# Normalising with scalar_tensor_tensor in place of tensor_scalar while GpSimd adds, in a matmul with batch normalisation

## The chip, the cores and the metric

The kernel runs on one core of one Trainium2 chip. The metric is the device time of an execution in microseconds (us). Most kernels here ran several times, in rounds with the kernel before on the same chip. The profiled execution has a span, from the first to the last instruction, that is about 2 us shorter than the time reported for it. SBUF and PSUM are the core's two on-chip memories; in the code, names that end in `_ps` lie in PSUM, where TensorE's results land, and the other tiles lie in SBUF. Positions such as "at 161.26" are us from the start of that span.

A run counts as fast unless it lies over 1.5% above the fastest of its kernel.

## The reference

```python
y = np.matmul(x, weight)                        # 16 x 512 rows, K = 1024, N = 768
mean = np.mean(y, axis=(0, 1), keepdims=True)   # per column, over all 8192 rows
var = np.var(y, axis=(0, 1), keepdims=True)
y_norm = (y - mean) / np.sqrt(var + eps)
return (gamma * y_norm + beta).astype(np.float32)
```

No output can be written before its column's statistics over all rows are known.

## The kernel before

The 768 columns are six tiles of 128. The first three tiles are finished first. Their outputs are then produced while TensorE still multiplies for the fourth, fifth and sixth. In that stretch, roughly 133 to 182 us, the engines share the work like this (a block is 1024 rows of a tile; in the fourth tile VectorE and ScalarE each normalise one half of it):

- TensorE: the remaining matmuls, with the transposes of finished output slotted between them one by one, in a fixed order.
- VectorE: batch statistics of each new block (`bn_stats`), the product of the first three tiles with their scale (`norm_rows`), and half of the normalising of the fourth tile (`norm` with "dve").
- GpSimd: the addition of the shift for the first three tiles (`shift_rows`), which reads two tensors in SBUF.
- ScalarE: copies out of PSUM and the other half of the fourth tile's normalising (`norm` with "act").

```python
def norm_rows(c, s):                      # VectorE, first three tiles
    ...
    seq(nc.vector.tensor_mul(             # the scale lies in PSUM
        o_sb, yrow[c][:, s:s + 2], aff[0][:, None, :].to_broadcast([P, 2, NA]),
    ))

def shift_rows(c, s):                     # GpSimd, first three tiles
    o_sb = ost["row", c, s]
    seq(nc.gpsimd.tensor_add(o_sb, o_sb, sum1[:, None, :].to_broadcast([P, 2, NA])))

def norm(nt, c, eng):                     # y = y * scale + shift, in place
    if eng == "act":
        ...
    else:
        seq((nc.vector if eng == "dve" else nc.gpsimd).tensor_scalar(
            y(nt, c), y(nt, c), scale[:, nt:nt + 1], shift[:, nt:nt + 1],
            op0=ALU.mult, op1=ALU.add,
        ))

def outputs(nt, t0, step):                # blocks of 1024 rows of tile nt
    for b in range(C // 2):
        tb = t0 + step * b
        ...
        for i in range(2):
            at(tb - 2.2 + 0.5 * i, norm, nt, 2 * b + i, "act" if tb < tr + 2.0 and i == 0 else "dve")
        ...                               # transposes, copy out, store
```

`seq` keeps each engine's instructions in the order of their planned times. `tr + 2.0` is, in planned time, shortly after GpSimd's last add.

## Time and profile before

| | before |
|---|---|
| time, median of the first three runs | 219.95 us (219.61 to 220.23) |
| span of the profiled execution | 217.6 us, granted TensorE clock 0.985 of full speed |
| busy: TensorE, VectorE, ScalarE, GpSimd | 92%, 72%, 56%, 62% |
| tensor_scalar of 128x512 (L382) | 43 of them, median 0.407 us, longest 3.38 |
| GpSimd's add of 128x768 (L289) | 24 of them, mean 1.87 us |

TensorE sets the pace over most of the kernel, VectorE between 157 and 176 us. An instruction that waits for a port is shown as busy for the whole wait. So the waits for GpSimd are not in the idle times at all, but in durations far above the median of the same instruction.

### The profile page before, as it was taken

The page shows a single profiled execution, that of the slowest core. Times are in us where ns is not written, and L with a number is a line of the kernel's source. Part 1 is how long each engine was busy: PE and PEld are TensorE (multiplying, and loading weights), DVE is VectorE, ACT ScalarE, POOL GpSimd, SP SyncE. Part 2 cuts the span into 40 slices and gives each one's busy share as a digit, 9 for nine tenths or more (in the row PEclk, how much of TensorE's full clock was granted, in tenths as well). Part 3 has the DMA queues.
Part 4 walks back from the last instruction along what each step waited for, and adds up shares of the span by engine and source line. Part 5 has one row for each costly group of instructions (what it writes and reads, how often), then busy time and mean ns, then how long its engine had stood idle before and what let it go on. Part 6 is the DMA issues. An engine that isn't in the chain of part 4 may idle for free.

```text
span 217.6 us, 3451 instructions
## 1 busy us (share of the span) xinstructions
PE 200.3 (92%) x1178; PEld 104.9 (48%) x1178; DVE 155.8 (72%) x263; ACT 121.2 (56%) x227; POOL 134.2 (62%) x153
## 2 busy tenths in 40 slices
PE   7997999999999999999999999999999979997900
PEld 2452555554544565645656545444444435554600
DVE  3222978887978789998654369988899999728900
ACT  2001463645543466645666414967866689976950
POOL 8887686878684699953558304999995963000000
PEclk9999999999999999999999999999999999999985
DMA  5999999999999999993000000897877989999998
GB/s 70 156 196 187 191 196 196 197 197 196 196 189 195 197 196 196 196 197 49 0 5 0 0 0 0 305 348 293 304 286 293 332 274 370 338 347 284 282 345 243
DMA packets 70161, 43.75 MB, mean 201 GB/s; under 512 B 4096, under 2 KB 69632, under 8 KB 70144
## 3 DMA queue, kind: packets, MB, share of 16 engines
q0 software_dynamic: 34624, 18.36, 61.6%
q1 hardware_dynamic: 35520, 25.18, 35.8%
q8 instruction: 9, 0.15, 0.3%
q14 instruction: 8, 0.07, 0.1%
HBM read 36.71 MB, written 25.17 MB: 284 GB/s over the span
## 4 chain that ended last, share of the span: by engine, by line
PE 75%; DVE 8%; DMA 5%; POOL 3%; issue 3%; ACT 2%; ACTq 1%; POOLq 0%
PE y_ps L196 39%; PE y_ps L186 29%; PE o_ps L398 5%; DMA w_sb<-in_weight_dram 3%; DMA ring<-in_x_dram 2%; DVE stats L316 2%; DVE y_sb L382 2%; DVE ring L283 2%; POOL w_sb L149 2%; DVE o_sb L283 1%; ACT o_sb L411 1%; POOL ring L162 1%; PE y_ps L330 1%; PE a_ps L272 1%; PE tot_ps L232 1%
## 5 line engine op out<-in xcount | busy, mean ns | idle before, releaser
L196 PE MATMUL y_ps<-xT_sb,w_sb 128*128 128x512 bf16 (+1 forms) x484 | 117.6, 381 | 1.6 <-DMA w_sb<-in_weight_dram 1.3
L196 PEld LDWEIGHTS <-w_sb 128*128 128x128 bf16 x484 | 45.9, 96 | 59.3 <-issue 3.1
L343 ACT CAST y_sb<-y_ps 128x512 bf16<-128x512 f32 x59 | 34.5, 585 | 53.7 <-DVE stats L316 50.7
L186 PE MATMUL y_ps<-w_sb,xT_sb 128*128 128x384 bf16 x384 | 63.4, 326 | 0.0
L316 DVE BATCH_NORM_STATS2 stats<-y_ps 128x6 f32<-128x512 f32 x58 | 39.3, 685 | 19.9 <-PE y_ps L196 19.9
L162 POOL DMA_DIRECT2D ring<-in_x_dram x72 | 45.2, 633 | 11.9 <-DVE xT_sb L174 6.5
L186 PEld LDWEIGHTS <-xT_sb 128*128 128x128 bf16 x384 | 37.5, 98 | 25.6
L212 POOL TENSOR_TENSOR sum<-sum,sq_sb 128x384 f32<-128x384 f32 x38 | 38.0, 1001 | 18.4 <-ACT sq_sb L208 17.1
L174 DVE STREAM_TRANSPOSE xT_sb<-ring 128x1024 f32<-128x1024 f32 (+1 forms) x34 | 39.5, 1168 | 12.8 <-DMA ring<-in_x_dram 12.8
L398 PE MATMUL o_ps<-ident,y_sb 128*128 128x128 bf16 x240 | 38.2, 219 | 3.6 <-DVE y_sb L382 2.5
L289 POOL TENSOR_TENSOR ring<-ring,sum 128x768 f32<-128x768 f32 x17 | 31.1, 1864 | 13.1 <-ACT sum L274 12.1
L215 DVE TENSOR_TENSOR sum<-y_ps,sum 128x384 f32<-128x384 f32 x48 | 26.1, 544 | 14.4 <-ACT sq_sb L208 13.4
L208 ACT ACTIVATE sq_sb<-y_ps 128x384 f32<-128x384 f32 x48 | 23.4, 492 | 15.2 <-PE y_ps L186 11.6
L221 ACT CAST y_sb<-y_ps 128x384 bf16<-128x384 f32 x48 | 22.9, 476 | 7.3 <-DVE sum L215 7.0
L411 ACT CAST ring<-o_ps 128x1024 f32<-128x1024 bf16 (+1 forms) x24 | 22.5, 951 | 4.2 <-PE o_ps L398 2.7
L398 PEld LDWEIGHTS <-y_sb 128*128 128x128 bf16 x240 | 19.4, 97 | 8.6 <-DVE y_sb L382 3.3
L382 DVE TENSOR_SCALAR y_sb<-y_sb,scale,shift 128x512 bf16<-128x512 bf16 x43 | 22.0, 565 | 0.0
L283 DVE TENSOR_TENSOR ring<-y_sb,a_ps 128x768 f32<-128x768 bf16 x17 | 15.9, 937 | 0.0
L289 POOL TENSOR_TENSOR o_sb<-o_sb,sum 128x768 f32<-128x768 f32 x7 | 13.2, 1880 | 2.9 <-DVE o_sb L283 2.9
L377 ACT ACTIVATE y_sb<-y_sb,shift,scale 128x512 bf16<-128x512 bf16 x17 | 13.5, 816 | 0.0
L155 PE MATMUL idle_ps<-idle_sb 128*128 128x512 bf16 x38 | 11.0, 456 | 1.2 <-DVE idle_sb L103 1.2
L411 ACT CAST o_sb<-o_ps 128x512 f32<-128x512 bf16 x16 | 7.9, 679 | 0.3 <-PE o_ps L398 0.3
(62 smaller groups left out, 50.1 us busy)
## 6 DMA issues: line engine op xcount, KB each, us to landing
ring<-in_x_dram POOLq DMA_DIRECT2D x56, 256.0 KB, 8.6
out_dram<-ring SPq DMA_DIRECT2D x25, 384.0 KB, 3.0
out_dram<-ring SPq DMA_DIRECT2D x16, 512.0 KB, 5.1
out_dram<-o_sb SPq DMA_DIRECT2D x16, 256.0 KB, 3.7
out_dram<-o_sb SPq DMA_DIRECT2D x7, 384.0 KB, 3.4
ring<-in_x_dram POOLq DMA_DIRECT2D x16, 128.0 KB, 5.3
w_sb<-in_weight_dram POOLq DMA_DIRECT2D x8, 96.0 KB, 4.6
w_sb<-in_weight_dram POOLq DMA_DIRECT2D x4, 192.0 KB, 5.6
```

Of the source, the lines that this page charges most:

```text
L162: seq(nc.gpsimd.dma_start(x_bf[32 * i:32 * i + 32], src[:, :, KQ * i:KQ * (i + 1)]))
L174: seq(nc.vector.transpose(dst[:, half, :, jw0:jw1], src[:, :, jw0:jw1]))
L186: seq(nc.tensor.matmul(y_ps, xT[c][:, jw, s * P:(s + 1) * P, e], w_sb[:, jw, e, 0:NA], start=(jw == 0 and e == 0), stop=(jw == JW - 1 and ...
L196: seq(nc.tensor.matmul(y_ps, w_sb[:, jw, e, nt * P:(nt + 1) * P], xT[c][:, jw, q0 * QR:q1 * QR, e], start=(jw == 0 and e == 0 and q0 == 0) ...
L212: seq(eng.tensor_add(acc, acc, py.pop(("sq", c, s))))
L215: seq(nc.vector.tensor_add(sum1, py["row", c, s][:, 0:NA], sum1))
L289: seq(nc.gpsimd.tensor_add(o_sb, o_sb, sum1[:, None, :].to_broadcast([P, 2, NA])))
L316: seq(nc.vector.bn_stats(stats_of(nt)[:, i, :], py[nt, c]))
L343: seq(nc.scalar.copy(y(nt, c), py.pop((nt, c))))
L382: seq((nc.vector if eng == "dve" else nc.gpsimd).tensor_scalar(y(nt, c), y(nt, c), scale[:, nt:nt + 1], shift[:, nt:nt + 1], op0=ALU.mult, ...
L398: seq(nc.tensor.transpose(dst, src, ident))
L411: seq(nc.scalar.copy(o_sb, src))
```

## The change

While GpSimd adds, a VectorE tensor_scalar waits for it. The prediction takes the tensor_scalar to run in a fast mode (0.40 us for 512 columns) and says where that comes from. The intent of the change is to leave that mode: the same arithmetic is written as a scalar_tensor_tensor, with the shift, one value per row, broadcast along the 512 columns as a second tensor.

```diff
+        elif eng == "dve1":
+            seq(nc.vector.scalar_tensor_tensor(
+                y(nt, c), y(nt, c), scale[:, nt:nt + 1],
+                shift[:, nt:nt + 1].to_broadcast([P, CH]), op0=ALU.mult, op1=ALU.add,
+            ))
 ...
-  at(tb - 2.2 + 0.5 * i, norm, nt, 2 * b + i, "act" if tb < tr + 2.0 and i == 0 else "dve")
+  at(tb - 2.2 + 0.5 * i, norm, nt, 2 * b + i, "dve" if tb > tr + 2.0 else "dve1" if i else "act")
```

Eight instructions change their form. No engine's order changes.

## The prediction

> **What bounds the kernel now.** The time before is 219.95 us; the profiled execution spans 217.6 us, and all positions below are us in that span. I read the page first: TensorE is busy in every slice from 10 to 199 us, VectorE is at nine tenths or more in the five slices from about 158 to 185 us, and the chain names PE for 75% and DVE for 8%. So TensorE paces the kernel, and VectorE must pace it for a stretch. The chain in order of time says where (start, duration, what):
>
> ```profile
> 154.79 2.05 PE y_ps L196 x9
> ...
> 161.34 1.58 DVE y_sb L382
> 162.92 1.64 issue
> ...
> 175.71 0.51 DVE mv L350
> ...
> 177.93 0.72 ACT y_sb L377
> 178.65 0.05 issue
> 178.69 0.23 PE o_ps L398
> ```
>
> The chain is on VectorE from 156.86 to 176.2 us, goes through the statistics aggregate (L350) to ScalarE and returns to TensorE at 178.69. From there it stays on TensorE, with no gap, to 199.37, where the last statistics begin. The "issue" of 1.64 us behind L382 is no issue: it lies inside one tensor_scalar, as the timelines of VectorE and GpSimd show (start, duration):
>
> ```profile
> 161.26 3.38 DVE L382 TENSOR_SCALAR y_sb<-y_sb,scale,shift 128x512 bf16<-128x512 bf16 x1
> 166.03 1.62 DVE L382 TENSOR_SCALAR y_sb<-y_sb,scale,shift 128x512 bf16<-128x512 bf16 x1
> 171.96 0.45 DVE L382 TENSOR_SCALAR y_sb<-y_sb,scale,shift 128x512 bf16<-128x512 bf16 x1
> 176.66 1.23 DVE L382 TENSOR_SCALAR y_sb<-y_sb,scale,shift 128x512 bf16<-128x512 bf16 x1
> ```
> ```profile
> 160.86 1.84 POOL L289 TENSOR_TENSOR o_sb<-o_sb,sum 128x768 f32<-128x768 f32 x1
> 162.65 1.84 POOL L289 TENSOR_TENSOR ring<-ring,sum 128x768 f32<-128x768 f32 x1
> 165.67 1.83 POOL L289 TENSOR_TENSOR o_sb<-o_sb,sum 128x768 f32<-128x768 f32 x1 [1.18 <-DVE o_sb L283]
> ```
>
> The same instruction takes a median of 0.407 us (its line's own view). The first one ends at 164.64, which is 0.15 after the second add's end (162.65 + 1.84 = 164.49); the next at 167.65, again 0.15 after 165.67 + 1.83 = 167.50. So a tensor_scalar that meets a GpSimd add waits for that add's end and then needs 0.15 us. The first one even let a second, already queued add go ahead. TensorE's own waits between 150 and 200 us show what all this can cost (total, times, longest):
>
> ```profile
> PE o_ps L398 <- ACT y_sb L377: 1.2, 2, 0.9
> PE o_ps L398 <- DVE y_sb L382: 0.8, 2, 0.5
> ```
>
> That is 1.97 us in four gaps (0.30, 0.50, 0.23, 0.94), all from 167 to 178.7.
>
> **What the skill says.** The Trainium skill, "SBUF — State Buffer", section "Who interferes with whom", says that VectorE and GpSimd share one pair of ports under an exclusive lock; a tensor_scalar in a two-port mode takes it, and so does a VectorE instruction with two SBUF inputs when the GpSimd instruction reads SBUF. The first half agrees with the lines above. For the second half the kernel before has a witness, the VectorE add of squares (L212), whose two inputs are both in SBUF. I looked for those that meet GpSimd's adds of the same line:
>
> ```profile
> 84.23 0.55 DVE L212 TENSOR_TENSOR sum<-sum,sq_sb 128x384 f32<-128x384 f32 x1
> 89.43 0.77 DVE L212 TENSOR_TENSOR sum<-sum,sq_sb 128x384 f32<-128x384 f32 x1
> 94.81 1.10 DVE L212 TENSOR_TENSOR sum<-sum,sq_sb 128x384 f32<-128x384 f32 x1
> ```
> ```profile
> 86.62 3.17 POOL L212 TENSOR_TENSOR sum<-sum,sq_sb 128x384 f32<-128x384 f32 x3
> 92.32 3.18 POOL L212 TENSOR_TENSOR sum<-sum,sq_sb 128x384 f32<-128x384 f32 x3
> ```
>
> Eight of the ten take 0.54 to 0.55 us. The two that start inside a GpSimd add end at 90.20 and 95.91, both 0.41 after GpSimd's end (89.79, 95.50). It is the same wait, and the 0.41 is the pass over 384 columns. "Vector Engine (DVE) Microarchitecture Reference", section "5.1 Performance modes — why throughput varies by op and dtype", enables the fast modes for copy, cast, tensor_scalar and tensor_tensor; scalar_tensor_tensor isn't in that list, and packing wants 16-bit operands throughout, while the broadcast shift is fp32. I take one column per cycle. No run shows that yet, as the scalar_tensor_tensors of before have one to three columns.
>
> **The change part by part.** It adds and removes no instruction. The queue orders of the two kernels are equal on all engines but for the form of eight VectorE instructions: i=1 of blocks 0 to 6 of the fourth tile, and i=1 of block 0 of the fifth, which also falls before the time test. In the trace of before these are the tensor_scalars at 161.26, 166.03, 169.90, 171.96, 173.80, 176.66 and two of the three merged at 179.31. They hold 6.9 us of waiting: (3.38 - 0.4) + (1.62 - 0.4) + (0.68 - 0.4) + 0.05 + 0.05 + (1.23 - 0.4) + (1.93 - 0.4). The change means to remove it, by leaving the two-port mode. It gives in1 a second SBUF stream instead, so I expect the wait to stay.
>
> Cost of the new form: tensor_tensor takes 0.544 us for 384 columns (L215) and 0.937 for 768 (L283), 1.02 ns a column, so 512 columns take 0.544 + 128 x 1.02 ns = 0.675 us free, against 0.40. Blocked, it ends 0.41 + 0.13 = 0.54 after GpSimd's add, against 0.15: 0.39 more.
>
> Then in VectorE's order, with an add of 1.83 us, and GpSimd's next add kept waiting while the new instruction holds the lock:
> Block 0: GpSimd's adds to 164.49 are as before; end 165.03 in place of 164.64, so +0.39.
> Block 1: its add (165.67) waits for the VectorE product in front, so it is itself 0.39 late; end +0.39 more, +0.78.
> Block 2: likewise, +1.17, 171.75. The GpSimd add behind it, which ran from 170.39 to 172.26, now starts its pass at about 171.75 and ends at 173.5.
> Block 3: before it lost only 0.05. Now it asks at about 173.15 and ends at 173.5 + 0.54 = 174.05 in place of 172.41, +1.64.
> Block 4: GpSimd's next add ends at about 174.05 + 1.8 = 175.85; end 176.4 in place of 174.25, +2.15.
> The aggregate (L350) thus starts at 177.8 in place of 175.64.
> Block 5: about 180.5 in place of 177.89; the last two end near 185 in place of 181.57, +3.3.
>
> On the path: block 0's delay mostly fits the slack of TensorE, whose transposes reach that data at about 165.0. Block 2's comes through whole (TensorE waits for it at 170.64), and the aggregate's +2.15 comes through ScalarE's queue to TensorE's restart: 178.69 becomes 180.8. Later blocks: the second half of block 6 is wanted at 183.15 + 2.15 = 185.3 and is there at about 184.9, so it just fits. TensorE has no gap from the restart to the last statistics, so +2.15 reaches them. Behind them lies a tail of fixed length: DMA is idle from 200.5 to 202.5 and then moves the last 16 stores. Sum: 219.95 + 2.1 = 222.05, rounded to 222.0.
>
> **The rivals.** First, no contention: with the shift read as one value a row, the second port may not count. Then each of the eight takes 0.68 and VectorE gains up to 6.9 - 8 x 0.275 = 4.7 us. But TensorE's gaps are only 1.97 us, and DMA is full from 180 to 200 us, so the end gains 1 to 2 us: 218 to 219. For it speaks the intent; against it the two blocked L212 adds. I give it 0.14.
> Second, the delay is absorbed: VectorE idles over 5 us between 188 and 196 and can catch up, which would leave 220 to 220.5. Against it: TensorE, not VectorE, carries the path after 178.69. I give it 0.12.
> Third, worse: a new instruction loses to two queued adds, as block 0's did (1.8 us each), or block 6 comes too late: 223.5 to 225. Before, four of the first five asked before the next add was ready, by as little as 0.08 us, so the order can tip. I give it 0.1.
>
> **Range and chances.** The main case has 0.64, at 221.3 to 222.8. With the rivals' weights 8 in 10 lie in 219.0 to 223.4. The 2% bounds are 215.55 and 224.35: faster would need more than TensorE's gaps hold, 0.01; slower needs the third rival in full, 0.04.
>
> **What would show it.** Right: no new instruction under 0.65 us; those that meet an add end about 0.54 after its end; the aggregate near 177.8, TensorE's restart near 180.8, its gaps near 4.1 us in all. Wrong at the root: instructions of 0.68 us lying inside GpSimd adds, with neither engine longer. Wrong in the size: waits as said, but TensorE's gaps grow by well under 2 us, or a new instruction spans two adds.

## The result, and the profile after

| | before | after |
|---|---|---|
| median of six runs each | 219.41 us | 221.64 us |
| lowest to highest | 218.31 to 220.23 | 220.56 to 222.64 |
| span of the profiled execution | 217.6 us | 220.2 us |

The ratio is 1.0104, with a 95% interval of 1.0059 to 1.0149. A ratio here is the mean time of one kernel's fast runs over that of the other's of the same rounds, so not quite the ratio of the medians. The change made the kernel slower by about 1%.

The chain of the changed kernel in order of time (start, duration, what) takes the same road as before:

```profile
154.88 2.50 PE y_ps L196 x11
...
161.90 1.58 DVE y_sb L383
163.47 2.05 issue
165.52 0.94 DVE o_sb L283
...
178.28 0.51 DVE mv L350
...
180.50 0.72 ACT y_sb L377
181.22 0.05 issue
181.26 0.23 PE o_ps L404
```

The two profiled executions are already 0.55 us apart before the first changed instruction: it starts at 161.81, against 161.26. That difference comes from the loading stage (the first batch statistics start at 20.91 against 20.37) and belongs to no changed line. Each comparison of positions has to take it off. The aggregate (L350) starts at 178.21 against 175.64, TensorE restarts at 181.26 against 178.69, and the last statistics start at 201.96 against 199.39. Each is 2.57 us later, or 2.02 us without the offset.

The new instructions on VectorE's timeline, and the GpSimd adds that they meet (start, duration):

```profile
161.81 3.79 DVE L383 SCALAR_TENSOR_TENSOR y_sb<-y_sb,scale,shift 128x512 bf16<-128x512 bf16 x1
166.99 2.01 DVE L383 SCALAR_TENSOR_TENSOR y_sb<-y_sb,scale,shift 128x512 bf16<-128x512 bf16 x1
173.71 0.86 DVE L383 SCALAR_TENSOR_TENSOR y_sb<-y_sb,scale,shift 128x512 bf16<-128x512 bf16 x1
```
```profile
163.21 1.83 POOL L289 TENSOR_TENSOR ring<-ring,sum 128x768 f32<-128x768 f32 x1
166.63 1.82 POOL L289 TENSOR_TENSOR o_sb<-o_sb,sum 128x768 f32<-128x768 f32 x1 [1.58 <-DVE o_sb L283]
171.74 2.29 POOL L289 TENSOR_TENSOR o_sb<-o_sb,sum 128x768 f32<-128x768 f32 x1
173.98 2.29 POOL L289 TENSOR_TENSOR ring<-ring,sum 128x768 f32<-128x768 f32 x1
```

The waits are still there. Add the durations to the starts: the three instructions end at 165.60, 169.00 and 174.57. The adds that they waited for end at 165.04, 168.45 and 174.03. The distance is 0.54 to 0.56 us, where the tensor_scalar ended 0.15 after its add. GpSimd now pays too: an add that begins while a new instruction is at work lasts up to 2.29 in place of 1.83 us, because it waits inside its own duration (beside tensor_scalars such adds took 1.87 to 2.00).

TensorE's waits of the changed kernel between 150 and 200 us (total, times, longest), to be held against the same two lines of before:

```profile
PE o_ps L404 <- ACT y_sb L377: 2.0, 2, 1.4
PE o_ps L404 <- DVE y_sb L383: 1.9, 2, 1.0
```

The four gaps (0.98, 0.90, 0.65 and 1.36) sum to 3.89 us, against 1.97. The difference of 1.92 is nearly the whole delay of 2.02.

### The profile page after: what moved, and what is told of

It is laid out like the page before. It is cut to its first block, busy times and chain, and to the rows that moved or that the text cites. A ratio compares the mean times of both kernels' runs of the same rounds, so it can differ in the third digit from the quotient of the medians.

```text
span 220.2 us, 3436 instructions
## 1 busy us (share of the span) xinstructions
PE 199.2 (90%) x1162; PEld 104.8 (48%) x1178; DVE 158.8 (72%) x263; ACT 120.9 (55%) x227; POOL 135.6 (62%) x153
## 4 chain that ended last, share of the span: by engine, by line
PE 73%; DVE 9%; DMA 5%; issue 3%; POOL 3%; ACT 2%; ACTq 1%; POOLq 0%
PE y_ps L196 38%; PE y_ps L186 28%; PE o_ps L404 5%; DMA w_sb<-in_weight_dram 3%; DMA ring<-in_x_dram 2%; DVE stats L316 2%; DVE y_sb L383 2%; DVE ring L283 2%; POOL w_sb L149 2%; DVE o_sb L283 1%; ACT o_sb L417 1%; POOL ring L162 1%; PE y_ps L330 1%; PE a_ps L272 1%; PE tot_ps L232 1%
## 5 line engine op out<-in xcount | busy, mean ns | idle before, releaser
L196 PE MATMUL y_ps<-xT_sb,w_sb 128*128 128x512 bf16 (+1 forms) x469 | 116.1, 381 | 3.0 <-DMA w_sb<-in_weight_dram 1.9
L343 ACT CAST y_sb<-y_ps 128x512 bf16<-128x512 f32 x59 | 35.1, 595 | 56.9 <-DVE stats L316 54.0
L289 POOL TENSOR_TENSOR o_sb<-o_sb,sum 128x768 f32<-128x768 f32 x7 | 14.1, 2012 | 3.8 <-DVE o_sb L283 3.8
L283 DVE TENSOR_TENSOR ring<-y_sb,a_ps 128x768 f32<-128x768 bf16 x17 | 15.9, 940 | 0.0
L383 DVE SCALAR_TENSOR_TENSOR y_sb<-y_sb,scale,shift 128x512 bf16<-128x512 bf16 x8 | 13.2, 1659 | 0.0
L388 DVE TENSOR_SCALAR y_sb<-y_sb,scale,shift 128x512 bf16<-128x512 bf16 x35 | 12.0, 409 | 0.0
```

What stands on the lines that cost most here:

```text
L196: seq(nc.tensor.matmul(y_ps, w_sb[:, jw, e, nt * P:(nt + 1) * P], xT[c][:, jw, q0 * QR:q1 * QR, e], start=(jw == 0 and e == 0 and q0 == 0) ...
L343: seq(nc.scalar.copy(y(nt, c), py.pop((nt, c))))
```

## The experiments

The theory, called the port theory in the expectations: the new form reads a second tensor from SBUF through the read port that VectorE shares with GpSimd, so it still waits for every add, and it then needs one cycle a column. The rivals: the wait has nothing to do with where the second input lies; or the cost is spread evenly over the eight instructions and comes from their slower pass. Kernels are compared only within the same rounds.

### e1: the shift in PSUM

The bank that holds the spread scale of the first three tiles has 128 spare columns. ScalarE writes the shift of the fourth and the fifth tile there as well, and the new form reads it from there.

```diff
+        aff["bank", i] = a_ps
 ...
+        seq(nc.scalar.activation(
+            aff["bank", 0][:, NA + nt:NA + nt + 1], mv[:, nt, 0:1], AF.Identity,
+            bias=beta_sb[:, one], scale=nscale))
 ...
-                shift[:, nt:nt + 1].to_broadcast([P, CH]), op0=ALU.mult, op1=ALU.add,
+                aff["bank", 0][:, NA + nt:NA + nt + 1].to_broadcast([P, CH]), op0=ALU.mult, op1=ALU.add,
```

> The changed kernel with the broadcast shift read from PSUM (a spare column of the bank that already holds the spread scale), so that the eight instructions have one SBUF input. Port theory: all eight take about 0.65 to 0.75 us even where they lie inside a GpSimd add, the adds stay near 1.83 us, the aggregate L351 comes 2 to 5 us earlier than in the changed kernel, TensorE's four gaps (3.9 us in the changed kernel) shrink below 1.5 us, and the time is 0.991 to 0.998 of the kernel before, so faster than both. Rival (the cost is the slow pass and a wait that any such instruction has beside GpSimd, wherever its input lies): instructions still spanning the adds, ratio 1.008 to 1.013 as for the change.

Measured: 218.87 us median against 219.95, ratio 0.995 (0.9918 to 0.9983), correct. The timelines of this run:

```profile
162.38 0.73 DVE L387 SCALAR_TENSOR_TENSOR y_sb<-y_sb,scale,a_ps 128x512 bf16<-128x512 bf16 x1
164.62 0.73 DVE L387 SCALAR_TENSOR_TENSOR y_sb<-y_sb,scale,a_ps 128x512 bf16<-128x512 bf16 x1
178.05 0.75 DVE L387 SCALAR_TENSOR_TENSOR y_sb<-y_sb,scale,a_ps 128x512 bf16<-128x512 bf16 x1 [2.82 <-ACT a_ps L361]
```
```profile
161.99 1.82 POOL L290 TENSOR_TENSOR o_sb<-o_sb,sum 128x768 f32<-128x768 f32 x1
163.78 1.83 POOL L290 TENSOR_TENSOR ring<-ring,sum 128x768 f32<-128x768 f32 x1
```

The same instruction, in the same place of the same order, now lies wholly inside a GpSimd add (162.38 to 163.11 inside 161.99 to 163.81), and neither engine is longer for it. All eight take 0.729 to 0.747 us. Apart from ScalarE's added writes, which e2 tests, only the place of one value per row is different, so the wait is bound to the second SBUF input. TensorE's gaps of 150 to 200 us fall to one of 0.37 us. The third line shows a wait that the edit brought in: VectorE stood 2.82 us until ScalarE's write for the fifth tile was done, although this instruction needs only the fourth tile's value. Both values lie in one PSUM buffer, and the instruction was made to wait for the earlier write to it. e5 takes this up.

### e2: the writes without the reading

Control: ScalarE's added writes stay, and the new form reads the shift from SBUF, as in the change. The lines are shown against e1.

```diff
-                aff["bank", 0][:, NA + nt:NA + nt + 1].to_broadcast([P, CH]), op0=ALU.mult, op1=ALU.add,
+                shift[:, nt:nt + 1].to_broadcast([P, CH]), op0=ALU.mult, op1=ALU.add,
```

> Control for the run before: the two added ScalarE writes of the shift to PSUM are there, but the eight instructions still read the shift from SBUF. Port theory: like the change, ratio 1.009 to 1.014, with the same waits for the GpSimd adds. If the added writes or the waits around them were what moves the time, this run would show the ratio of the run before instead.

Measured: 222.46 us, ratio 1.0122 (1.0084 to 1.0159). The waits for GpSimd are those of the changed kernel: the first new instruction lasts 3.76 us, and the gaps on TensorE sum to 3.87. The added writes did not make e1 fast. They even cost something: a VectorE product (L284), which reads the same PSUM buffer, stood 0.69 us until the second write was done.

### e3 and e4: which of the eight cost time

e3 keeps the first five in the new form, e4 the other three.

```diff
-  "dve" if tb > tr + 2.0 else "dve1" if i else "act"
+  "dve" if tb > tr + 2.0 else ("dve1" if nt == GA and b < 5 else "dve") if i else "act"     # e3
+  "dve" if tb > tr + 2.0 else ("dve" if nt == GA and b < 5 else "dve1") if i else "act"     # e4
```

> Only blocks 0 to 4 of the fourth tile in the new form, the last three back as tensor_scalar. By the predicted path the whole cost comes from these five: ratio 1.008 to 1.012, aggregate about 2 us late. Rival (every instruction costs the same): five eighths of 1.04%, 1.0065.

> Only the last three (block 5, block 0 of the fifth tile, block 6) in the new form. By the predicted path they fit TensorE's slack: ratio 0.998 to 1.002, TensorE's gaps near 2.0 us as before. Rival (every instruction costs the same): three eighths of 1.04%, 1.004.

Measured: e3 221.83 us, ratio 1.0081 (1.0046 to 1.0117); e4 220.11 us, ratio 1.0011 (0.9978 to 1.0045). The interval of e3 holds both 1.010 and 1.0065, so the times alone don't decide. The traces do. TensorE's waits of e3, then of e4:

```profile
PE o_ps L404 <- ACT y_sb L377: 2.0, 2, 1.3
PE o_ps L404 <- DVE y_sb L383: 1.9, 2, 1.0
```
```profile
PE o_ps L404 <- ACT y_sb L377: 1.2, 2, 0.9
PE o_ps L404 <- DVE y_sb L388: 0.8, 2, 0.5
```

e3 has the gaps of the changed kernel and e4 those of the kernel before. A better measure than the whole time is the stretch from the start of block 0's normalising to the start of the last statistics, since it leaves out the loading stage, where executions differ:

| | stretch | us | against before |
|---|---|---|---|
| before | 161.26 to 199.39 | 38.13 | |
| after | 161.81 to 201.96 | 40.15 | +2.02 |
| e3, first five | 161.84 to 201.95 | 40.11 | +1.98 |
| e4, last three | 161.73 to 199.86 | 38.13 | 0.00 |
| e2, writes alone | 162.23 to 202.85 | 40.62 | +2.49 |
| e1, all from PSUM | 162.38 to 198.80 | 36.42 | -1.71 |

The first five carry the whole cost and the last three none, though in e4 the last two also wait, and take 2.98 us together. From the end of the stretch to the end of the span it is 18.2 us before and after, so the tail is no part of the change. e2 is 0.47 longer than the changed kernel, all of it behind TensorE's restart; that the 0.69 us above caused it is likely but not shown.

### e5: the shift in PSUM for the fourth tile alone

The second write is dropped, and block 0 of the fifth tile is a tensor_scalar again (the first line is shown against e1).

```diff
+        if nt == GA:                      # around the added write
 ...
-  "dve" if tb > tr + 2.0 else "dve1" if i else "act"
+  "dve" if tb > tr + 2.0 else ("dve1" if nt == GA else "dve") if i else "act"
```

> The shift from PSUM for the fourth tile alone: no second ScalarE write, and block 0 of the fifth tile is a tensor_scalar again. In the run with all eight, VectorE stood 2.8 us at block 5 for that second write. Port theory: that stand goes, the instructions stay near 0.74 us, TensorE's gap of 0.37 us before 180 us goes, ratio 0.990 to 0.996. If the wait on the write cost nothing because TensorE is the bound, the ratio stays at 0.995.

Measured: 217.07 us median, ratio 0.9898 (0.9862 to 0.9934). One of the six executions took 1166.85 us and is not among the fast ones. VectorE no longer stands still at block 5, and TensorE has no gap between 150 and 196 us; the view of waits is empty. The stretch is 161.59 to 197.10, 35.51 us, 2.62 less than before. That is 0.65 more than TensorE's gaps of before (1.97), and it shows how those gaps are to be read. In this part a matmul is drawn 0.39 us long, while the next instruction can start 0.23 after it, so its last 0.16 holds up nothing. By this estimate each gap is drawn 0.16 too short: 1.97 + 4 x 0.16 = 2.61. For the changed kernel it comes out as 3.89 + 0.64 = 4.53, and its stretch is 4.64 longer than that of e5.

### e6: the new form with nothing beside it

The sixteen normalisings of the last tile, after GpSimd's last add, take the new form too.

```diff
-            at(tb - 1.2, norm, nt, c, "dve")
+            at(tb - 1.2, norm, nt, c, "dve1")
```

> The changed kernel with the last tile's sixteen tensor_scalars in the new form too, after GpSimd's last add, to measure the form with both inputs in SBUF and nothing beside it: 0.675 us each by the prediction's estimate, 0.73 to 0.75 if it costs what it costs with the shift in PSUM. The time is expected within 1 us of the changed kernel, because the last stores, not VectorE, set the pace there.

Measured in one look: 221.66 us, correct. The view of the line gives the shortest, median and longest duration in ns:

```profile
L383 DVE SCALAR_TENSOR_TENSOR y_sb<-y_sb,scale,shift x24: 742/744/3782, 161.5 to 213.1; 128x512 bf16<-128x512 bf16 x24
```

Free, the form takes 0.744 us (median), not 0.675. In a row, sixteen take 10.69 us (0.66 apart), against 5.25 before. One time says little, but the trace does: from the start of the last statistics to the end of the span it is 18.2 us (201.60 to 219.8), as in the changed kernel (201.96 to 220.2). VectorE's speed is not what sets the end there.

### e7 and e8: GpSimd writes and reads nothing

Each add of GpSimd becomes two memsets of the same tile, in the kernel before (e7) and in the changed one (e8). Their outputs are wrong, which doesn't matter for the times.

```diff
-        seq(nc.gpsimd.tensor_add(o_sb, o_sb, sum1[:, None, :].to_broadcast([P, 2, NA])))
+        for _ in range(2):
+            seq(nc.gpsimd.memset(o_sb, 1.0))
```

> The kernel before with each GpSimd add replaced by two memsets of the same tile, which write SBUF and read nothing (wrong result on purpose). If the two-port tensor_scalar needs the shared write port too, those that meet a memset end about 0.15 us after it, longer than 0.45 us; if only reads are shared, all take 0.40 us.

> The changed kernel with the same memsets in place of the adds (wrong result on purpose). Port theory in the skill's wording (two SBUF inputs contend with GpSimd's reads only): all eight take their free time, 0.67 to 0.75 us, also inside memsets. Rival (any GpSimd instruction holds the pair against it): those that meet a memset end 0.54 us after it.

Measured, one look each: 218.0 us (e7) and 216.54 us (e8). A memset takes 0.738 us. A tensor_scalar of e7 and the pair of memsets that it meets:

```profile
167.04 1.03 DVE L383 TENSOR_SCALAR y_sb<-y_sb,scale,shift 128x512 bf16<-128x512 bf16 x1
```
```profile
167.18 1.56 POOL L290 MEMSET o_sb<- 128x768 f32 x2
```

A new instruction of e8 and its pair:

```profile
170.65 0.75 DVE L384 SCALAR_TENSOR_TENSOR y_sb<-y_sb,scale,shift 128x512 bf16<-128x512 bf16 x1
```
```profile
170.79 1.53 POOL L290 MEMSET o_sb<- 128x768 f32 x2 [0.72 <-DVE o_sb L283]
```

The tensor_scalar waits for the first memset (167.18 + 0.74 = 167.92) and ends at 168.07, 0.15 later. Two others of e7 take 1.02 us in the same way, and one that starts inside a memset (164.16, the memset from 163.73) ends 0.15 after it too (164.62 against 164.47). The new form, in the same position, takes 0.75, and all eight lie between 0.733 and 0.751. In these lines the VectorE instruction is drawn as the first to start, so they alone could mean that it went first. Another of e8 starts in the middle of a memset and is no longer:

```profile
163.26 0.74 DVE L384 SCALAR_TENSOR_TENSOR y_sb<-y_sb,scale,shift 128x512 bf16<-128x512 bf16 x1
```
```profile
162.77 1.53 POOL L290 MEMSET o_sb<- 128x768 f32 x2
```

So the two forms share different things with GpSimd. The tensor_scalar waits even for an instruction that only writes. The new form does not; it waits for the kernel's adds, which also read SBUF. A GpSimd instruction with a single SBUF input was not tried.

### e9 and e10: the two faster versions on one chip

e9 is e5 again, e10 is e1 again, unchanged.

> The version with the shift from PSUM for the fourth tile alone, once more, because one of its six executions took 1166.85 us and because it was not compared with the version for all eight on one chip. If the long execution belongs to the kernel it comes again; else all lie within 1% of each other, at a ratio of 0.987 to 0.993.

> The version with all eight from PSUM, on the same chip. By TensorE's gap before 180 us alone (0.37 us shown, about 0.5 true) it should be 0.2% to 0.3% slower than the run beside it; the two earlier ratios lie 0.5% apart, with intervals that touch.

Measured: e9 216.90 us, ratio 0.9891 (0.9848 to 0.9934); e10 217.16 us, ratio 0.9899 (0.9866 to 0.9932). The long execution did not come back, and its cause is unknown. The two versions are not told apart by time: 0.3 us between the medians, with ranges that overlap (215.91 to 218.42, 216.94 to 218.55). In the traces the stretch is 35.51 us in e9, as in e5, and 36.43 in e10 (36.42 in e1). The stretches repeat to a hundredth; the whole times don't, and e10 came out 0.5% better than e1 against the kernel before. In these two pairs, what differs between executions of one kernel lies outside the stretch.

## Why the prediction was right

- "I expect the wait to stay": right. e1 and e2 differ only in whether the shift is read from PSUM or SBUF, and the waits come and go with that. e8 adds that a GpSimd instruction which only writes is no hindrance.
- The 0.54 after the add's end: 0.54 to 0.56 in the profile after. The two blocked adds of squares in the kernel before were enough to get this from.
- Block by block, taking the offset of 0.55 off the measured ends: 165.05, 168.45, 171.78, 174.02 and 176.27, where the working had 165.03, 168.43 (167.65 + 0.78), 171.75, 174.05 and 176.4. The aggregate was +2.02 late, not +2.15. The working let GpSimd's next add begin after the new instruction's end; the profile has it begin during that instruction, waiting inside its own duration, and be done up to 0.1 us earlier. Block 5 came at 180.28 (180.5 expected) and the last two at 184.65 (near 185).
- The path: TensorE's restart +2.02 (2.1 expected), block 5 and the two after it within the slack (e4: 0.00), gaps of 3.89 in all (4.1 expected).
- The free duration was mis-sized: 0.744 in e6, against 0.675 scaled from tensor_tensor. It did no harm, because the first six met an add, and the blocked ends count from the add. That the same scaling missed the free duration and met the blocked end is partly luck. One column per cycle was not tested: every new instruction has 512 columns.
- The first rival, no contention, was refuted for this form, and its size was too small: "TensorE's gaps are only 1.97 us" took the drawn gaps at face value. Without contention (e5, e9) the stretch gains 2.62 us and the time 1.0 to 1.1%, more than the 1 to 2 us that the rival allowed with DMA full.
- The second rival falls with e3 and e4: the delay of the first five comes through whole.
- The third rival did not occur. Apart from block 0, which lost to two adds in both kernels, no new instruction in the trace lost to a second one. That a queued add goes ahead is seen, not tested. One order fits the changed kernel's trace: the add that went ahead (163.21) had its product (L283) done at 161.29, before the new instruction started at 161.81; the adds behind blocks 2, 3 and 4, which waited, had theirs at 171.33, 173.79 and 176.03, each 0.07 to 0.08 after the new instruction's start.

The time has a share that no changed line explains: about 0.55 us of the two profiled spans' difference of 2.6. The stretch, +2.02, is the better figure for the change, and the interval of the ratio, 1.3 to 3.3 us of 219.3, holds it.

## What to carry to other kernels

To keep VectorE clear of GpSimd, ask of each VectorE instruction how many SBUF tensors it reads, and not only whether it is in a fast mode; a broadcast of one value per row counts as a tensor. If the second operand can lie in PSUM, a slower pass that never waits can beat a fast one that does: 0.74 against 0.40 us an instruction, and yet 1% less time for the kernel. Port waits stand inside the durations of both engines, so look for instructions far above the median of their own kind.

## What the Trainium skill lacked or had wrong

- "SBUF — State Buffer", section "Who interferes with whom", says that a VectorE instruction with two SBUF inputs contends with a GpSimd instruction that reads SBUF and not with one that only writes it. The runs agree: waits up to 3.79 us beside adds, 0.733 to 0.751 us beside memsets (e8). It does not say that a broadcast of a single value per row counts as the second input; it does (the change, against e1).
- The same section says that whoever issues first gets the pair. Block 0's instruction was issued at 161.26 in the kernel before, waited for the add in flight, and then let a second add, started at 162.65, go ahead as well: 3.38 us in all, and 3.79 in the changed kernel. No page describes how queued GpSimd instructions stand in the order.
- "VectorE: DVE Perf Modes", section "The perf-mode tier table (the rule you actually need)", has no row for scalar_tensor_tensor. Measured free at 128x512, with bf16 data and an fp32 broadcast: 0.744 us with the broadcast in SBUF, 0.73 to 0.75 with it in PSUM, against 0.40 for the bf16 tensor_scalar.
- "SBUF — State Buffer" names the lock but no page says where the profile shows the wait: it is counted as busy time of the instruction that waits, on VectorE (0.40 becomes 3.38 us) as on GpSimd (1.83 becomes 2.29 us).
